# The first inner tile's weights loaded alone ahead of x's first tile, the second's behind it, and four idle products instead of five

## The chip, the core and the metric

The kernel runs on one core of one Trainium2 chip. The metric is the device time of one execution in microseconds (us). Five engines work side by side, each through its own fixed list of instructions and in that order: TensorE (PE; its weight loads are listed as PEld), VectorE (DVE), ScalarE (ACT), GpSimd (POOL) and SyncE (SP, which here only issues DMAs). They wait for each other with semaphores. TensorE's clock has two levels, 1.2 and 2.4 GHz.

## What is computed

One layer of a decoder over 1024 tokens of width 1024 in fp32. Only its beginning matters here:

```
h = _rmsnorm(r, attn_norm[i]).astype(dt)
z = h @ w_in[i]
aq, af, ai, ag, bq, bk, bv, cq, ck, cv, cg = jnp.split(z, SPLITS, axis=-1)
hd = lambda t: t.reshape(b, s, -1, HEAD_DIM)
ya = _hgrn2(hd(aq), hd(af), hd(ai), hd(ag), lb_all[i], hgrn_gnorm[i])
yb = _swa_sinks(hd(bq), hd(bk), hd(bv), attn_sinks[i], cos, sin)
yc = _retention(hd(cq), hd(ck), hd(cv), hd(cg), cos, sin)
...
r = r + mix @ w_out[i]
r = r + _conv_ffn(h2, w_gate[i], w_up[i], conv_w[i], conv_b[i], w_down[i])
```

`_hgrn2` is a gated linear recurrence over the tokens. Behind these come a gated per-layer embedding and a last norm.

## The kernel before

Every large fp32 product is made of three products of rounded halves (`mm3`, lines 113 to 117): weight high by x high (L115), weight high by x low (L116), weight low by x high (L117). A "high" half is a copy into the type fp32r, made by ACT; the "low" half is the difference, made by DVE. One product takes 128x128 weights against 512 tokens.

**The start.** The projection's columns are cut into 22 tiles (`FT`), of which the first three (af0, aq0, ai0) are computed while x arrives. x is transposed, eight inner tiles `x0` to `x7` of 128 x 1024, each loaded in two halves of 512 tokens (256 KB each) by SP. The weights of these three column tiles come in pairs of inner tiles (`w_first`, four DMAs of 384 KB, `wr_s0` to `wr_s6`), each ahead of its pair of x tiles on SP's queue. Of each x tile ACT makes `xh` (times the norm's gain, which lies in `small`, loaded on ACT's queue), DVE makes `xl`, ACT the squares for the norm, and TensorE then makes 18 products: 3 column tiles x 2 halves x 3. The order of the code within this loop is:

```
if k % 2 == 0:
    raw = ap.tile([P, 2, NS * P], F32, ...)
    nc.sync.dma_start(raw, a["w_first"][k // 2])
for h in range(2):
    nc.sync.dma_start(x[:, half(h)], a["xT"][k][:, half(h)])
if k % 2 == 0:
    wh, wl = split_w(raw, [P, 2, NS * P], f"s{k}")
for h in range(2):
    S.mul(hi[:, half(h)], x[:, half(h)], col(C_G1 + k))
```

Ahead of it TensorE multiplies a zeroed tile (`idle`, L209); one such fp32 product is two passes in the trace. A DMA takes one of eight semaphore lanes; an issuing engine waits until the lane's DMA before has landed.

**Behind it.** The sum of squares (`ss_x`) goes through a reciprocal root on DVE, is spread by TensorE (`rb_x`) and copied by ACT in two halves into `rs1` (L185). Then the other column tiles follow one by one (`project`, L254: load, `wh_` on ACT, `wl_` on DVE, 48 products), and between them the products of the recurrence (`hgrn`, from L437): seven levels n, each for two token halves h. A level's four products (`level`, L458, tiles `l{j}{n}{h}`, so `l011` is part 0, level 1, half 1) read `q` and `k`; then DVE selects the scores (L466), multiplies q (L482) and k (L483), and k so multiplied is what the next level of that half reads. The tables of the rotary embedding (`rope_tables`: L509 to L526, `ang`, `angn`, `sinT`, `cosT`) are laid between the levels. A product's result lies in one of three PSUM buffers (`pg`), which is free for the next column tile once DVE has read it.

The order on each engine comes from a scheduler with a model of its own that looks at the whole program; the code's order and priorities are its input.

Of the kernel before, what the change touches and what calls it, by code (L numbers as in the profile page):

```python
# [17 lines left out]
F32 = mybir.dt.float32  # L18
F32R = mybir.dt.float32r
# [3 lines left out]
ALU = mybir.AluOpType  # L23
# [3 lines left out]
P = 128  # L27
# [14 lines left out]
NS = 3  # L42
# [31 lines left out]
def trunk(ctx: ExitStack, tc: tile.TileContext, a, out, out_end, dbg):  # L74
    nc = tc.nc
    V, S, G, TE = nc.vector, nc.scalar, nc.gpsimd, nc.tensor
# [3 lines left out]
    wp = ctx.enter_context(tc.tile_pool(name="wp", bufs=2))  # L80
# [9 lines left out]
    def b1(name):  # L90
        return ps.tile([P, H2], F32, tag="b1", bufs=5, name=name)

    def half(h):
        return slice(h * H2, (h + 1) * H2)
# [5 lines left out]
    def split_w(raw, shape, name, e=V):  # L100
        hi = wp.tile(shape, F32R, tag="whi", bufs=2, name=f"wh_{name}")
        S.copy(hi, raw)
        lo = wp.tile(shape, F32R, tag="wlo", bufs=2, name=f"wl_{name}")
        e.tensor_tensor(out=lo, in0=raw, in1=hi.bitcast(F32), op=ALU.subtract)
        return hi, lo
# [7 lines left out]
    def mm3(o, wh, wl, xh, xl, first, last, on=False):  # L113

        TE.matmul(o, wh, xh, start=first, stop=False, skip_group_check=on)  # L115
        TE.matmul(o, wh, xl, start=False, stop=False, skip_group_check=on)  # L116
        TE.matmul(o, wl, xh, start=False, stop=last, skip_group_check=on)  # L117
# [8 lines left out]
    def col(i):  # L126
        return small[:, i:i + 1]
# [77 lines left out]
    idle = ap.tile([P, H2], F32, tag="st", bufs=2, name="idle")  # L205
    V.memset(idle, 0.0)
    pt = b1("idle")
    for _ in range(5):
        TE.matmul(pt[:, :256], idle[:, :P], idle[:, :256], start=True, stop=True)  # L209
    S.dma_start(small, a["small"])  # L210
    with tc.high_priority(offset=100000):
        xs = [ap.tile([P, T], F32, tag="zg", bufs=4, name=f"x{k}") for k in range(4)]
        xs += [ap.tile([P, T], F32, tag=t, bufs=1, name=f"x{4 + k}") for k, t in enumerate(("ob", "zo"))]
        both = ap.tile([P, 2, T], F32, tag="ob2", bufs=1, name="x67")
        xs += [both[:, k, :] for k in range(2)]
        for k in range(KD):
            x = xs[k]
            hi = big.tile([P, T], F32R, tag="big", name=f"xh{k}")
            lo = big.tile([P, T], F32R, tag="big", name=f"xl{k}")
            if k % 2 == 0:  # L220
                raw = ap.tile([P, 2, NS * P], F32, tag=("s0", "s1", "kt", "zt")[k // 2], bufs=1, name=f"wr_s{k}")
                nc.sync.dma_start(raw, a["w_first"][k // 2])
            for h in range(2):
                nc.sync.dma_start(x[:, half(h)], a["xT"][k][:, half(h)])
            if k % 2 == 0:
                wh, wl = split_w(raw, [P, 2, NS * P], f"s{k}")
            for h in range(2):
                S.mul(hi[:, half(h)], x[:, half(h)], col(C_G1 + k))
                V.scalar_tensor_tensor(out=lo[:, half(h)], in0=x[:, half(h)], scalar=col(C_G1 + k),
                                       in1=hi[:, half(h)].bitcast(F32), op0=ALU.mult, op1=ALU.subtract)  # L230
            if k == 0:
                S.square(acc, x)
            else:
                sq = ap.tile([P, T], F32, tag="zv", bufs=2, name=f"sq{k}")
                S.square(sq, x)
                V.tensor_tensor(out=acc, in0=acc, in1=sq, op=ALU.add)
            xh.append(hi)
            xl.append(lo)
            for n in range(NS):
                for h in range(2):  # L240
                    w = slice(n * P, n * P + P)
                    mm3(first[n][h], wh[:, k % 2, w], wl[:, k % 2, w], hi[:, half(h)], lo[:, half(h)],
                        k == 0, k == KD - 1)
# [166 lines left out]
    def hgrn_f(j, of):  # L410
        f = zt(f"f{j}", "zf", 1)
        k = zt(f"k{j}", "zk", 2)
        scaled(f, of)
        S.activation(k, f, AF.Sigmoid, scale=-1.0)
        S.activation(f, f, AF.Sigmoid)
        V.tensor_scalar(out=k, in0=k, scalar1=oml[:, j:j + 1], scalar2=None, op0=ALU.mult)
        V.tensor_scalar(out=f, in0=f, scalar1=oml[:, j:j + 1], scalar2=lbt[:, j:j + 1], op0=ALU.mult, op1=ALU.add)
        return f, k
# [293 lines left out]
    f, k = hgrn_f(0, first[0])  # L712
# [5 lines left out]
    f, k = got["af1"]  # L718
# [49 lines left out]
    def f4(tag, name, shape=(P, T), dt=F32):  # L768
        if tag == "big":
            return big.tile(list(shape), dt, tag="big", name=name)  # L770
        if tag in ("wraw", "whi", "wlo"):
            return wp.tile(list(shape), dt, tag=tag, bufs=1 if tag == "wraw" else 2, name=name)
        return fp.tile(list(shape), dt, tag=tag, bufs=BUFS[tag], name=name)
# [125 lines left out]
    def weights_up_1(f):  # L899

        if f == 1:
            g = cp.tile([P, T], F32, tag="rs", bufs=1, name="wg1")
        else:
            g = f4("ws" if f == 2 else "w5" if f > 2 and f % 2 else "wraw", f"wg{f}")
        nc.sync.dma_start(g.rearrange("p (k c) -> p k c", k=KD), a["w_gu"][f, 0])
        hi, lo = [f4(t, f"{t}g{f}", dt=F32R) for t in ("whi", "wlo")]
        hl(hi, lo, g)
        return g, {n + 1: (hi[:, half(n)], lo[:, half(n)]) for n in range(2)}
# [138 lines left out]
    with tc.high_priority(offset=3000):  # L1047
        raw, A0 = weights_up_1(0)
# [5 lines left out]
    with tc.high_priority(offset=3000):  # L1054
        raw, A1 = weights_up_1(1)
# [23 lines left out]
    for f in range(3, NF):  # L1079
        with tc.high_priority(offset=3000):  # L1080
            raw, A = weights_up_1(f)
# [190 lines left out]
    for n in range(NC // 2):  # L1272
# [7 lines left out]
        for i, (d0, d1) in enumerate(groups):  # L1280
# [8 lines left out]
            t = f4("big", f"et{n}{i}")[:, :d1 - d0]  # L1289
# [138 lines left out]
```

## Time and profile before

| | |
|---|---|
| median of 3 runs | 1246.35 us (1245.96 to 1246.54) |
| the profiled execution | 1246.38 us |
| its span, first to last instruction | 1244.6 us |
| TensorE busy | 1225.4 us, 98% of the span |
| VectorE busy | 892.2 us, 72% |
| ScalarE busy | 543.8 us, 44% |
| mean granted clock of TensorE | 0.998 of full speed |

Times in the trace count from the first instruction. "Idle before" an instruction and what ended it stand in brackets. In a row with xN, N instructions were merged, the duration runs from the first's start to the last's end, and the name loses its numbers (`z_af` is any half of af0 or af1).

### The profile page before, as it was taken

To read this page: it belongs to the slowest core of one execution; us is meant where nothing else is said; L and a number is where in the kernel's file an instruction comes from. 1 tells how busy PE (TensorE), PEld (TensorE's weight loads), DVE (VectorE), ACT (ScalarE), POOL (GpSimd) and SP (SyncE) were. 2 spreads that over 40 slices of the span, in tenths; PEclk is the share of its full clock that TensorE was granted. 3 is DMA by queue.
4 is the path that set the end of the run, shared out by engine and by line. 5 is a ranking of instruction groups with operands and counts; after the bars stand their busy time and mean duration, and the time that the engine had idled before them with its cause. 6 is when DMAs were issued, how large, how long until landed. Compare 5 with 4: busy or idle time off the path is not lost.

```text
span 1244.6 us, 15889 instructions
## 1 busy us (share of the span) xinstructions
PE 1225.4 (98%) x6030; PEld 1023.5 (82%) x6030; DVE 892.2 (72%) x1510; ACT 543.8 (44%) x838; POOL 126.7 (10%) x158
## 2 busy tenths in 40 slices
PE   9999999999999999999999999999999999999997
PEld 7888888887888888887788888888888888888886
DVE  7996967557777476987878887787667675566374
ACT  7324233247766344754343334433335353444332
POOL 2000000011210313100111111111101000000000
PEclk9999999999999999999999999999999999999999
DMA  7100110110001944333554544544579786443131
GB/s 258 51 23 29 35 34 18 34 34 34 24 29 46 353 127 166 121 94 127 177 177 152 179 130 154 182 160 154 191 265 339 272 290 207 144 152 119 34 135 68
DMA packets 59964, 165.53 MB, mean 133 GB/s; under 512 B 6320, under 2 KB 6832, under 8 KB 59888
## 3 DMA queue, kind: packets, MB, share of 16 engines
q1 hardware_dynamic: 42608, 106.71, 25.6%
q0 software_dynamic: 15552, 55.84, 13.2%
q10 hardware_dynamic: 1728, 1.97, 0.5%
q8 instruction: 47, 0.77, 0.3%
q14 instruction: 29, 0.24, 0.1%
HBM read 120.20 MB, written 44.30 MB: 132 GB/s over the span
## 4 chain that ended last, share of the span: by engine, by line
PE 51%; DVE 1%; DMA 0%; issue 0%; ACT 0%; DVEq 0%
PE d L116 6%; PE d L115 6%; PE d L117 6%; PE gb L116 5%; PE gb L117 5%; PE gb L115 5%; PE gd L117 3%; PE gd L115 3%; PE gd L116 3%; PE ga L116 1%; PE ga L117 1%; PE ga L115 1%; PE pe L117 1%; PE pg L115 1%; PE pe L115 1%; PE pe L116 1%
## 5 line engine op out<-in xcount | busy, mean ns | idle before, releaser
L115 PE MATMUL d<-hhd,hwd 128*128 128x512 f32 x308 | 119.8, 389 | 0.0
L116 PE MATMUL d<-lhd,hwd 128*128 128x512 f32 x308 | 119.8, 389 | 0.0
L117 PE MATMUL d<-hhd,lwd 128*128 128x512 f32 x308 | 119.8, 389 | 0.0
L781 DVE TENSOR_TENSOR lwd<-wdr,hwd 128x1024 fp32r<-128x1024 f32 (+1 forms) x39 | 47.0, 1209 | 36.9 <-ACT hwd L780 36.8
L780 ACT CAST hwd<-wdr 128x1024 fp32r<-128x1024 f32 (+1 forms) x39 | 40.5, 1039 | 72.8 <-PE d L116 59.0
L115 PE MATMUL gd<-b,f 128*128 128x512 f32 x176 | 68.8, 391 | 1.4 <-ACT us L964 1.4
L115 PE MATMUL gb<-b,hf 128*128 128x512 f32 x176 | 68.7, 390 | 0.1
L116 PE MATMUL gd<-b,f 128*128 128x512 f32 x176 | 68.5, 389 | 0.0
L117 PE MATMUL gd<-b,f 128*128 128x512 f32 x176 | 68.5, 389 | 0.0
L116 PE MATMUL gb<-b,hf 128*128 128x512 f32 x176 | 68.5, 389 | 0.0
L117 PE MATMUL gb<-b,lf 128*128 128x512 f32 x176 | 68.3, 389 | 0.0
L115 PEld LDWEIGHTS d<-hhd,hwd 128*128 128x128 f32 x308 | 57.8, 188 | 12.1
L117 PEld LDWEIGHTS d<-hhd,lwd 128*128 128x128 f32 x308 | 57.8, 188 | 12.1
L116 PEld LDWEIGHTS d<-lhd,hwd 128*128 128x128 f32 x308 | 57.8, 188 | 11.8
L781 DVE TENSOR_TENSOR lhd<-hr,hhd 128x1024 fp32r<-128x1024 f32 (+1 forms) x39 | 46.7, 1207 | 6.7 <-ACT hhd L780 6.5
L780 ACT CAST hhd<-hr 128x1024 fp32r<-128x1024 f32 (+1 forms) x39 | 39.8, 1034 | 20.1 <-DMA hr<-tad 11.0
L780 ACT CAST f<-wg 128x512 fp32r<-128x512 f32 x22 | 13.7, 624 | 77.7 <-PE gd L117 77.7
L781 DVE TENSOR_TENSOR f<-s,f 128x1024 fp32r<-128x1024 f32 x22 | 26.9, 1224 | 28.3 <-ACT f L780 28.3
L780 ACT CAST f<-s 128x1024 fp32r<-128x1024 f32 x22 | 23.1, 1050 | 50.3 <-PE gb L117 46.5
L115 PEld LDWEIGHTS gd<-b,f 128*128 128x128 f32 x176 | 33.0, 188 | 9.3 <-ACT us L964 2.5
L115 PEld LDWEIGHTS gb<-b,hf 128*128 128x128 f32 x176 | 33.0, 188 | 7.7 <-ACT gs L964 0.5
L971 DVE SCALAR_TENSOR_TENSOR cv<-gs,small,cv 128x1023 f32<-128x1023 f32 x22 | 28.2, 1284 | 15.1 <-ACT cv L970 15.1
(491 smaller groups left out, 3506.1 us busy)
## 6 DMA issues: line engine op xcount, KB each, us to landing
wg<-w_gu SPq DMA_DIRECT2D x22, 512.0 KB, 4.4
wu<-w_gu SPq DMA_DIRECT2D x22, 512.0 KB, 3.5
sd<-w_dn POOLq DMA_DIRECT2D x22, 512.0 KB, 5.2
sd<-sd POOLq DMA_DIRECT2D x22, 512.0 KB, 3.9
wdr<-sd SPq DMA_DIRECT2D x44, 256.0 KB, 3.7
wr_wo<-w_out SPq DMA_DIRECT2D x16, 512.0 KB, 3.7
wdr<-w_dn SPq DMA_DIRECT2D x15, 512.0 KB, 4.8
hod<-us POOLq DMA_DIRECT2D x11, 512.0 KB, 2.9
```

Of the source, the lines that this page charges most:

```text
L115: TE.matmul(o, wh, xh, start=first, stop=False, skip_group_check=on)
L116: TE.matmul(o, wh, xl, start=False, stop=False, skip_group_check=on)
L117: TE.matmul(o, wl, xh, start=False, stop=last, skip_group_check=on)
L780: S.copy(hi, src)
L781: return e.tensor_tensor(out=lo, in0=src, in1=hi.bitcast(F32), op=ALU.subtract)
L971: V.scalar_tensor_tensor(out=cv[:, 1:], in0=gs[:, :T - 1], scalar=w(1), in1=cv[:, 1:], op0=ALU.mult, op1=ALU.add)
```

## The change

Of the first pair of weights only tile 0's part (192 KB) is loaded ahead of `x0`, and tile 1's part ahead of `x1`; the high and low halves of these two parts are made apart, each at its own tile's turn. The other three pairs stay as they are. TensorE makes four idle products instead of five. From here on a line has a number that is nine higher.

```
-    for _ in range(5):
+    for _ in range(4):
         TE.matmul(pt[:, :256], idle[:, :P], idle[:, :256], start=True, stop=True)
...
+            if k < 2:
+                nc.sync.dma_start(raw[:, k, :], a["w_first"][0][:, k, :])
+            elif k % 2 == 0:
                 nc.sync.dma_start(raw, a["w_first"][k // 2])
             for h in range(2):
                 nc.sync.dma_start(x[:, half(h)], a["xT"][k][:, half(h)])
-            if k % 2 == 0:
+            if k == 0:
+                wh, wl = [wp.tile([P, 2, NS * P], F32R, tag=t, bufs=2, name=f"{t}_s0") for t in ("whi", "wlo")]
+            if k < 2:
+                S.copy(wh[:, k, :], raw[:, k, :])
+                V.tensor_tensor(out=wl[:, k, :], in0=raw[:, k, :], in1=wh[:, k, :].bitcast(F32), op=ALU.subtract)
+            elif k % 2 == 0:
                 wh, wl = split_w(raw, [P, 2, NS * P], f"s{k}")
```

The scheduler answers with other orders in a few places. At the start SP's list was (in brackets the lanes it waits for; `DMAHW0` is the lane of `small`, `DMAHW1` that of `wr_s0`):

```order
L222 DMA wr_s0_110<-w_first 128x768
L224 DMA x0_101<-xT 128x512 x2
L224 DMA x1_102<-xT 128x512 x2
L222 DMA wr_s2_172<-w_first 128x768 [waits DMAHW1_49]
L224 DMA x2_103<-xT 128x512 [waits DMAHW2_49]
```

and is now:

```order
L224 DMA wr_s0_109<-w_first 128x384
L228 DMA x0_100<-xT 128x512 x2
L224 DMA wr_s0_109<-w_first 128x384
L228 DMA x1_101<-xT 128x512
L228 DMA x1_101<-xT 128x512 [waits DMAHW0_49]
L226 DMA wr_s2_174<-w_first 128x768 [waits DMAHW1_49]
L228 DMA x2_102<-xT 128x512 [waits DMAHW2_49]
```

So x1's second half stands behind a wait for `small`. On TensorE the first products were:

```order
L209 MATMUL idle_94<-idle_92 128x256 x5
L115 MATMUL z_af00_85<-xh0_108,wh_s0_114 128x512
L116 MATMUL z_af00_85<-xl0_109,wh_s0_114 128x512
L117 MATMUL z_af00_85<-xh0_108,wl_s0_116 128x512
L115 MATMUL z_af01_86<-xh0_108,wh_s0_114 128x512
L115 MATMUL z_aq00_87<-xh0_108,wh_s0_114 128x512
L116 MATMUL z_aq00_87<-xl0_109,wh_s0_114 128x512
L117 MATMUL z_aq00_87<-xh0_108,wl_s0_116 128x512
L116 MATMUL z_af01_86<-xl0_109,wh_s0_114 128x512
```

and are now (`z_af00` is the first token half of af0, `z_af01` the second):

```order
L209 MATMUL idle_94<-idle_92 128x256 x4
L115 MATMUL z_af00_85<-xh0_107,whi_s0_113 128x512
L115 MATMUL z_af01_86<-xh0_107,whi_s0_113 128x512
L116 MATMUL z_af00_85<-xl0_108,whi_s0_113 128x512
L117 MATMUL z_af00_85<-xh0_107,wlo_s0_114 128x512
L115 MATMUL z_aq00_87<-xh0_107,whi_s0_113 128x512
L116 MATMUL z_af01_86<-xl0_108,whi_s0_113 128x512
```

The second product is now the one that needs the second half of `xh0`, ahead of the one that needs `xl0`. On ACT the mask `rmask` is issued some 20 rows later than before, and in the place behind the norm's sum the high half of af1's weights, which stood ahead of both copies into `rs1`, stands between them:

```order
L517 DMA posi_721<-pos 128x1024
L185 COPY rs1_70<-rb_x_410 128x512
L102 CAST wh_af1_443<-wr_af1_441 128x1024
L185 COPY rs1_70<-rb_x_416 128x512
L423 ACT_TABLE_LOAD
```

The third place is among the first levels of the recurrence. TensorE's list there was:

```order
L458 MATMUL l001_574<-q0_431,k0_424 128x128 x4
L458 MATMUL l010_596<-q0_431,k0_424 128x128 x3
L115 MATMUL z_aq11_539<-xh0_108,wh_aq1_534 128x512
...
L117 MATMUL z_aq11_539<-xh7_333,wl_aq1_536 128x512
L458 MATMUL l011_625<-q0_431,k0_424 128x128 x4
L458 MATMUL l020_635<-q0_431,k0_424 128x128 x4
L115 MATMUL z_ai10_651<-xh0_108,wh_ai1_647 128x512
```

and is now:

```order
L467 MATMUL l001_576<-q0_433,k0_426 128x128 x4
L467 MATMUL l010_598<-q0_433,k0_426 128x128 x4
L467 MATMUL l011_627<-q0_433,k0_426 128x128 x4
L115 MATMUL z_aq11_541<-xh0_107,wh_aq1_536 128x512
...
L117 MATMUL z_aq11_541<-xh7_335,wl_aq1_538 128x512
L467 MATMUL l020_637<-q0_433,k0_426 128x128 x4
L115 MATMUL z_ai10_653<-xh0_107,wh_ai1_649 128x512
```

`l011` has moved from behind the 24 products of `z_aq11` to ahead of them. DVE's list in that place is now (`k0` behind `l001` is what `l011` reads; the buffer that `z_aq11` takes is the one that the first `f1` row frees, where before it was the one that two `q1` rows ahead of `l001`'s selection freed):

```order
L475 COPY_PREDICATED sa01_507<-lmask_75,l000_554 128x256
L491 TENSOR_TENSOR q0_433<-q0_433,f0_425 128x512
L492 TENSOR_TENSOR k0_426<-k0_426,f0_425 128x256
L535 TENSOR_TENSOR sinT_385<-sinT_385,rs1_70 128x1024
L438 TENSOR_TENSOR q1_620<-z_aq10_540,rs1_70 64x512
L475 COPY_PREDICATED sa00_506<-lmask_75,l001_576 128x256
L475 COPY_PREDICATED sa01_507<-lmask_75,l001_576 128x256
L491 TENSOR_TENSOR q0_433<-q0_433,f0_425 128x512
L492 TENSOR_TENSOR k0_426<-k0_426,f0_425 128x256
L475 COPY_PREDICATED sa00_506<-lmask_75,l010_598 128x128x2
L299 TENSOR_TENSOR f1_497<-z_af10_447,rs1_70 128x512
```

Before, two `q1` rows stood in place of `sinT` and one `q1`, and `sinT` had come earlier. Two more moves on DVE lie ahead of this: of the four rows L516 (`ang`) two stood ahead of `f0` and two behind it, and now it is one and three; and `angn` (L522) stands ahead of `l000`'s selection now, not behind `l001`'s. Behind it, the rows `wl_ag0`, `cosT` and the two `q1` of `z_aq11` stood ahead of `l011`'s multiplication of `k0` and stand behind it now. From some 30 rows further on the engines' lists are the same.

## Rows read from the trace of the kernel before

**Rows 1.** The page's part 1: busy time, share of the span and number of instructions of each engine.

```profile
PE 1225.4 (98%) x6030; PEld 1023.5 (82%) x6030; DVE 892.2 (72%) x1510; ACT 543.8 (44%) x838; POOL 126.7 (10%) x158
```

**Rows 2.** The view of waits for TensorE over the whole span, one of its longest: who waited for whom, us in total, times, longest.

```profile
PE l L458 <- DVE k L483: 1.4, 2, 0.8
```

**Rows 3.** The timeline of the first 10 us: start, duration, engine (SPq and ACTq are the issue of DMAs), line, operation, out<-in. The first x row is x0's first half; the pair at 1.67 begins with x0's second half, the pair at 2.13 is x1's.

```profile
0.74 0.41 ACTq L210 DMA_DIRECT2D small<-small  x1
1.20 0.42 SPq L224 DMA_DIRECT2D x<-xT  x1
1.67 0.90 SPq L224 DMA_DIRECT2D x<-xT  x2
2.13 0.91 SPq L224 DMA_DIRECT2D x<-xT  x2
...
4.14 0.83 ACT L102 CAST wh_s<-wr_s 128x768 fp32r<-128x768 f32 x1 [1.46 <-DMA wr_s<-w_first]
5.14 0.72 ACT L228 ACTIVATE xh<-x,small 128x512 fp32r<-128x512 f32 x1 [0.17 <-DMA x<-xT]
5.91 0.50 PE L115 MATMUL z_af<-xh,wh_s 128*128 128x512 f32 x1 [0.46 <-ACT xh L228]
6.33 0.72 ACT L228 ACTIVATE xh<-x,small 128x512 fp32r<-128x512 f32 x1 [0.46 <-DMA x<-xT]
6.70 0.49 PE L116 MATMUL z_af<-xl,wh_s 128*128 128x512 f32 x1 [0.29 <-DVE xl L229]
7.04 0.40 PE L117 MATMUL z_af<-xh,wl_s 128*128 128x512 f32 x1
7.08 0.75 DVE L229 SCALAR_TENSOR_TENSOR xl<-x,small,xh 128x512 fp32r<-128x512 f32 x1 [0.43 <-ACT xh L228]
7.27 0.40 PE L115 MATMUL z_af<-xh,wh_s 128*128 128x512 f32 x1
```

**Rows 4.** From issue to landing, us: the DMAs issued around 0.7 to 1.25 us (KB each, last column), then x0's second half alone, then all of x's up to 20 us.

```profile
wr_s<-w_first SPq DMA_DIRECT2D x1, 384.0 KB, 3.4
x<-xT SPq DMA_DIRECT2D x1, 256.0 KB, 3.9
...
small<-small ACTq DMA_DIRECT2D x1, 62.0 KB, 3.6
...
DMA to landing us min/median/max: 4.6/4.6/4.6
...
DMA to landing us min/median/max: 3.9/5.5/6.1
```

**Rows 5.** A stretch of the start: from:to us, length, busy us of the engines, granted clock, DMA share, GB/s.

```profile
8.00:9.00 1.00, 1.00 (x6) 0.84 (x5) 0.35 (x1) 1.00 (x2) 0.00 (x0) 1.00 1.04 374
```

**Rows 6.** The passes of the idle products in narrow windows of the timeline; each row begins with the start of the first pass that runs in its window.

```profile
4.18 0.84 PE L209 MATMUL idle<-idle 128*128 128x256 f32 x2
4.61 0.84 PE L209 MATMUL idle<-idle 128*128 128x256 f32 x3
4.86 0.59 PE L209 MATMUL idle<-idle 128*128 128x256 f32 x2
```

**Rows 7.** The timeline of ACT and DVE behind the norm's sum.

```profile
32.85 1.04 ACT L102 CAST wh_af<-wr_af 128x1024 fp32r<-128x1024 f32 x1 [6.84 <-PE z_ai L116]
33.93 1.23 DVE L104 TENSOR_TENSOR wl_af<-wr_af,wh_af 128x1024 fp32r<-128x1024 f32 x1 [0.93 <-ACT wh_af L102]
34.18 0.59 ACT L185 COPY rs<-rb_x 128x512 f32<-128x512 f32 x1 [0.28 <-PE rb_x L173]
38.04 2.49 DVE L516 SCALAR_TENSOR_TENSOR ang<-angn,ang 128x1024 f32<-128x1024 f32 x2
42.59 1.37 DVE L290 TENSOR_TENSOR ai<-z_ai,rs 128x512 f32<-128x512 f32 x2 [0.27 <-PE z_ai L117]
```

**Rows 8.** The timeline of DVE at the first levels.

```profile
55.23 0.69 DVE L447 TENSOR_TENSOR sa<-l0d,ident 128x512 f32<-128x512 f32 x1 [1.41 <-PE l0d L446]
55.84 1.22 DVE L526 TENSOR_TENSOR sinT<-sinT,rs 128x1024 f32<-128x1024 f32 x1
63.91 0.41 DVE L483 TENSOR_TENSOR k<-k,f 128x256 f32<-128x256 f32 x1
64.24 1.38 DVE L429 TENSOR_TENSOR q<-z_aq,rs 64x512 f32<-64x512 f32 x2
67.41 0.41 DVE L483 TENSOR_TENSOR k<-k,f 128x256 f32<-128x256 f32 x1
```

**Rows 9.** The timeline of TensorE in the same stretch (the number behind the x counts passes: an fp32 product has two; a product's start to the next one's is its pace).

```profile
60.07 1.15 PE L458 MATMUL l<-q,k 128*128 128x128 f32 x8 [0.23 <-DVE q L472]
63.80 1.75 PE L458 MATMUL l<-q,k 128*128 128x128 f32 x14
65.77 0.47 PE L115 MATMUL z_aq<-xh,wh_aq 128*128 128x512 f32 x1 [0.22 <-DVE q L429]
73.31 0.48 PE L115 MATMUL z_ai<-xh,wh_ai 128*128 128x512 f32 x1
78.90 1.16 PE L458 MATMUL l<-q,k 128*128 128x128 f32 x8 [0.79 <-DVE k L483]
81.64 0.47 PE L115 MATMUL z_ai<-xh,wh_ai 128*128 128x512 f32 x1
```

**Rows 10.** The view of waits for DVE from 380 to 604 us, its longest row.

```profile
DVE r L827 <- PE o L117: 29.6, 10, 3.4
```

## The prediction

> **What bounds the kernel now.** I read the page's busy shares first, then TensorE's waits, then the timelines at the places where the order of instructions differs. TensorE is busy for 1225.4 of 1244.6 us [rows 1], so the time is that of its list plus its waits: about 19 us, of which some 6 lie ahead of the first product that counts. The longest later one is short: 1.4 us in two waits for DVE's multiplication of k [rows 2]. What moves TensorE's stream therefore moves the end, unless a later wait shrinks or grows with it. In the start the reader is to see three steps: the weights land and are cast at 4.14, x0's first half lets `xh` start at 5.14 and the first product at 5.91, x0's second half lets `xh` start only at 6.33 [rows 3]. From the third product at 7.04 on the stream runs without a gap, one product in 0.23 us (7.04 to 7.27). The tiles behind are no limit: 18 products take 18 x 0.227 = 4.1 us, a tile of x and its weights (704 KB) at the 374 GB/s of [rows 5] 1.9 us.
>
> **The start, part by part.** (1) *192 KB less ahead of x0.* x0's second half was issued at 1.67 and landed 4.6 later, at 6.27 [rows 3, 4]. How much earlier it lands no row shows. Upper bound: the first half landed at 5.1 (issued at 1.20, plus 3.9), 0.95 behind the weights' 4.14; at that pace 192 KB are worth 0.71 us. Lower bound: nothing, if the 4.6 us are a latency of issue. By the rate of 374 GB/s they are 196.6 / 374 = 0.53. I take 0.55, since the rate is that of a busy queue and this queue is busy: 5.72. From `xh`'s start to its product took 0.77 (5.14 to 5.91), and 0.06 lay between landing and start (6.27 to 6.33), so the product that needs the second half of `xh0` can run at 5.72 + 0.06 + 0.77 = 6.55. It now stands second on TensorE, so the third comes 0.34 later (6.70 to 7.04 in rows 3) at 6.89, against 7.04. **Gain 0.15.** `xl0` of the first half is ready before that: `xh` moves from 5.14 to about 4.6, product and `xl` with it, since the smaller cast (384 columns for 768, half of 0.83 us) ends at about 4.1; `small` lands at 0.74 + 3.6 = 4.34 [rows 3, 4] and is no later. The sixth product needs `xl0` of the second half: `xh` ends at 6.50, `xl` takes 0.75, 7.28; TensorE comes there at 6.89 + 3 x 0.23 = 7.58. The bounds give the third product at 6.73 (gain 0.31) and at 7.44 (loss 0.40). A loss is possible since before only the fourth product needed that half, and three ran ahead of it.
>
> The Trainium skill's page "DMA: Bandwidth & Descriptors", section "Anatomy of one DMA — SWDGE (gpsimd) path", puts a DMA at a fixed part of about 2 us plus its bytes at 436 GB/s, with the fixed part mostly the wait for the last write's receipt. By it 196.6 KB less are worth 0.45 us and the gain of the start would be 0.05; my 0.55 goes by this case's rows.
>
> (2) *The second part of the weights ahead of x1, and x1's second half behind a wait.* SP issued all of x1 by 2.13 + 0.91 = 3.04 [rows 3]; now the second half waits for `small`, 4.34. With the 3.9 to 6.1 us of [rows 4] it lands at 8.3 to 10.4. Its `xh` is wanted by the fourth product of the next tile, 6.89 + 15 x 0.227 + 0.23 + 3 x 0.23 = 11.2, its `xl` at 11.5: landing by about 9.9 hides it. Cost 0, at most 0.5. What SP issues behind it waits for lanes that free earlier than before (weights, x0), and `rmask`'s 256 KB leave this stretch.
>
> (3) *Four idle products.* Their passes start 0.43 apart to 4.61, then 0.25 [rows 6]: the step from 1.2 to 2.4 GHz falls between, while the eighth pass (the fourth product's last) runs. Four products reach to about 5.0, so the step still falls into them; 0.
>
> **Behind the norm's sum.** Now `rs1`'s first copy, 34.18 to about 34.7, precedes the cast of `wh_af1`, which stood at 32.85. So `wl_af1` moves from 33.93 to 34.7 + 1.04 + 0.04 = 35.8, DVE is 1.85 late [rows 7]. One L516 less ahead of `f0` gives back 1.2, the 0.27 us wait ahead of `ai` the most of a third: 0.3 late. TensorE wants `wh_af1` only after 36 products from 34.8 on, at 43: hidden, with 6 us to spare. The third L516 behind `f0` adds 1.14.
>
> **The levels.** DVE finished the preparations at 53.8 (55.23 less the wait of 1.41) and will do so at 53.8 + 0.3 + 1.14 = 55.25. There it no longer waits for TensorE, and neither the first `sa` nor `sinT` (1.13) stand ahead of `wl_ai`: `wl_ai` 1.14, two `sa` 1.2, q 1.13, two `sa` 1.2, q 1.13, `angn` 0.6, selection 1.09 and q 0.65 bring it to `k0` of `l000` at 63.4 (63.91 before). Then `sinT` 1.13 and one `q1` 0.61 stand where two `q1` took 1.42, so `k0` behind `l001`, which started at 67.41 and took 0.41, starts at about 67.2 and ends at 67.6 [rows 8]. **Unchanged, but wanted earlier**: `l011` reads it, and stands now right behind `l010`. TensorE comes there early: `l000` no longer waits (60.07 becomes 59.7), 12 products from 60.6 end at 63.4, `l001` and `l010` at 0.215 a product end at 65.15. **`l011` waits 2.45 us**, to 67.6, and ends at 68.5; `z_aq11` waits further until the first `f1` has freed its buffer (67.55, selection 0.55, `f1` 0.69): 68.8 for 65.77 [rows 9].
>
> What comes back: 24 products without the odd `l010` take 5.6 us, to 74.4, then 4 products of `l020` (0.86) instead of 8 bring `z_ai10` to 75.3, for 73.31: 2.0 late. At 78.90 TensorE waited 0.79 us for `k0` of `l011`, behind a DVE that had `cosT`, `wl_ag0` and two `q1` ahead of it; these stand behind it now, it ends at about 75.0, and `l021` starts at 75.3 + 2.8 = 78.1 with no wait. `l021` 0.87, 12 products 2.83, `l030` 0.85: `z_ai11` at 82.65, for 81.64. **Loss 1.0.** Both chains hang on TensorE's start alike, so the 0.15 stays a term of its own. Behind 90 us the lists are the same, and DVE waits for TensorE again and again (ten times for `o` alone, 29.6 us [rows 10]), so a shift of TensorE shifts its partners; later waits give nothing back.
>
> **Sum.** Against the profiled execution's own 1246.38 us (span 1244.6, 1.78 around it; median of the runs 1246.35): 1246.38 - 0.15 + 1.0 = 1247.2 us.
>
> **Rivals.** (A) *The forecast*, 55%. (B) *x0's second half lands no earlier*, the 4.6 us being latency: loss 0.4 in the start, 1247.8. For it: it landed 1.17 behind the first half, while the weights were 0.95 ahead of that. Against: the queue is full. 14%. (C) *DVE is ahead at the levels*: were it over 2.5 us earlier, `l011` would not wait, `z_aq11`'s wait would go too, and the 0.23, 0.22 and 0.79 us of waits in [rows 9] would be partly gone: some 0.7 less than before, and with the 0.15 of the start 1245.5. Against: DVE has 1.41 us of waiting to give in that stretch and 1.14 of new work ahead of it. 16%. (D) *DVE is a microsecond later* (the cast of `wh_ai1`, or `sinT` waiting for ACT): it comes in full, 1248.2. 9%. (E) *The clock falls back*: with one idle product less TensorE does one product between 5.0 and 6.55, and if that cost it the upper level, products take twice 0.227 us; from about seven such products on (7 x 0.23 = 1.6 us on top of the forecast) the kernel is slower by over 0.2%. With eight: 1247.2 + 1.8 = 1249.0. Against: before it stood 0.46 and 0.29 us without a loss of pace. 6%. The page "TensorE: Matmul & The Clock Gate", section "What's actually happening" in the Trainium skill, says the clock is held down by default and released by activity; by it (E) is possible, and the pace of [rows 6] agrees that activity released it here.
>
> **Numbers.** Runs of one kernel spread here by 0.6 us; 0.2% is 2.5 us, which is what a measurement can tell from no change. Predicted: 1247.2 (A). The range from 1245.4 to 1248.5 takes in A to D with their bounds and leaves out E and the ends. Faster by over 0.2% (under 1243.9): 2%, what C with both upper bounds would still miss. Slower (over 1248.9): 7%, E and the end of D. Within 0.2%: 91%.
>
> **What would show it.** Right: the third product at about 6.9; the cast of the first weights near 3.6; a wait of about 2.4 us of `l011` for DVE's k near 65 and a short one of `z_aq11` for `f1`; no wait at `l021`; `z_ai11` about 0.85 later than 81.64; the same waits as before behind 90 us. Wrong: a third product behind 7.04 (B), a pace over 0.23 there (E), no wait at `l011` (C), or later waits that shrink by what was lost.

## The result, and the profile after

| | before | after |
|---|---|---|
| median of 20 runs each | 1246.53 us (1245.61 to 1249.91) | 1248.12 us (1246.52 to 1252.08) |
| span of the profiled execution | 1244.6 us | 1246.2 us |
| ratio after to before | | 1.0015, 95% interval 1.0009 to 1.0021 |

The changed kernel is 1.6 us slower, within 0.2%. The forecast was 1247.2 us, so 0.8 us of loss was seen ahead and 0.8 was not. TensorE has as much work as before [rows 1]: two passes fewer, and 1.4 us more that a slower pace at the start makes. The new wait is the one that was forecast: 2.3 us in place of the longer of the two waits that make up the 1.4 us of [rows 2]; the other, 0.65 at 140 us, is still there. The page's part 1 and the view of TensorE's waits (us in total, times, longest):

```profile
PE 1226.8 (98%) x6028; PEld 1024.8 (82%) x6028; DVE 892.4 (72%) x1511; ACT 543.7 (44%) x839; POOL 126.7 (10%) x158
```

```profile
PE l L467 <- DVE k L492: 3.0, 2, 2.3
```

The start in the timeline (start, duration, engine, line, operation, out<-in; in brackets the idle time ahead and what ended it), the counterpart of [rows 3]:

```profile
3.46 0.51 ACT L232 CAST whi_s<-wr_s 128x384 fp32r<-128x384 f32 x1 [0.78 <-DMA wr_s<-w_first]
4.47 0.72 ACT L237 ACTIVATE xh<-x,small 128x512 fp32r<-128x512 f32 x1 [0.50 <-DMA x<-xT]
5.24 0.80 PE L115 MATMUL z_af<-xh,whi_s 128*128 128x512 f32 x1
5.54 0.72 ACT L237 ACTIVATE xh<-x,small 128x512 fp32r<-128x512 f32 x1 [0.35 <-DMA x<-xT]
6.32 0.79 PE L115 MATMUL z_af<-xh,whi_s 128*128 128x512 f32 x1 [0.28 <-ACT xh L237]
6.91 0.63 PE L116 MATMUL z_af<-xl,whi_s 128*128 128x512 f32 x1
7.34 0.63 PE L117 MATMUL z_af<-xh,wlo_s 128*128 128x512 f32 x1
...
9.47 0.63 PE L117 MATMUL z_aq<-xh,wlo_s 128*128 128x512 f32 x1
9.90 0.47 PE L115 MATMUL z_aq<-xh,whi_s 128*128 128x512 f32 x1
10.20 0.40 PE L116 MATMUL z_aq<-xl,whi_s 128*128 128x512 f32 x1
10.44 0.39 PE L117 MATMUL z_aq<-xh,wlo_s 128*128 128x512 f32 x1
```

Loads and casts are earlier, as meant: the second half's `xh` starts at 5.54 for 6.33. But from 6.91 to 9.90 the seven products stand 0.43 us apart, where before they stood 0.23 apart from 7.04 on [rows 3]. Products stand as far apart where the clock column reads 0.50 (69.68 to 70.11 in the second run with five idle products, below), so this is the pace of the lower of the two clock levels, and 7 x 0.2 = 1.4 us of loss. The third product at 6.91 looks like the forecast's 6.89, but by the pace of [rows 3] (0.34 behind the second) it would have been 6.66. The view by stretches does not show the lower level here: its clock column (the 1.00 ahead of the DMA share) is as high as in [rows 5], yet x3 stands where x6 stood:

```profile
8.00:9.00 1.00, 1.00 (x3) 0.76 (x3) 0.93 (x3) 1.00 (x3) 0.00 (x0) 1.00 0.98 363
```

The levels on TensorE, against [rows 9], with the very last product:

```profile
61.03 1.07 PE L467 MATMUL l<-q,k 128*128 128x128 f32 x8
64.68 1.98 PE L467 MATMUL l<-q,k 128*128 128x128 f32 x16
68.96 1.15 PE L467 MATMUL l<-q,k 128*128 128x128 f32 x8 [2.31 <-DVE k L492]
70.02 0.50 PE L115 MATMUL z_aq<-xh,wh_aq 128*128 128x512 f32 x1
76.41 0.48 PE L115 MATMUL z_ai<-xh,wh_ai 128*128 128x512 f32 x1
79.25 1.05 PE L467 MATMUL l<-q,k 128*128 128x128 f32 x8
83.70 0.48 PE L115 MATMUL z_ai<-xh,wh_ai 128*128 128x512 f32 x1
...
1237.14 0.28 PE L117 MATMUL pe<-hpg,lp 128*128 128x256 f32 x1
```

And DVE, against [rows 7, 8]:

```profile
37.09 1.23 DVE L104 TENSOR_TENSOR wl_af<-wr_af,wh_af 128x1024 fp32r<-128x1024 f32 x1 [2.29 <-ACT wh_af L102]
...
68.41 0.40 DVE L492 TENSOR_TENSOR k<-k,f 128x256 f32<-128x256 f32 x1
69.25 1.31 DVE L299 TENSOR_TENSOR f<-z_af,rs 128x512 f32<-128x512 f32 x2
```

This splits the profiled difference. Ahead of the levels TensorE is 1.19 us late (61.03 against 60.07 less its wait of 0.23). Behind them `z_ai11` is 2.06 late (83.70 against 81.64), so **the levels cost 0.87**. The last product (1235.13 before) is 2.01 late: nothing is given back in between. The tail behind it, on other engines, was 0.4 shorter in this execution, which leaves the 1.6 of the spans. So 1.2 us are the start's, where the forecast had a gain of 0.15. The rows of the kernel before for the norm's sum and for the last product are:

```profile
29.05 1.84 PE L159 MATMUL ss_x<-ones,acc 128*128 128x1 f32 x16
...
1235.13 0.28 PE L117 MATMUL pe<-hpg,lp 128*128 128x256 f32 x1
```

### The profile page after: what moved, and what is told of

Read it like the earlier page. It is cut to its first block, busy times and chain, and to the rows that moved or that the text cites. A ratio compares the mean times of both kernels' runs of the same rounds, so it can differ in the third digit from the quotient of the medians.

```text
span 1246.2 us, 15891 instructions
## 1 busy us (share of the span) xinstructions
PE 1226.8 (98%) x6028; PEld 1024.8 (82%) x6028; DVE 892.4 (72%) x1511; ACT 543.7 (44%) x839; POOL 126.7 (10%) x158
## 4 chain that ended last, share of the span: by engine, by line
PE 51%; DVE 1%; DMA 0%; issue 0%; ACT 0%; DVEq 0%
PE d L117 6%; PE d L116 6%; PE d L115 6%; PE gb L115 5%; PE gb L117 5%; PE gb L116 5%; PE gd L115 3%; PE gd L117 3%; PE gd L116 3%; PE ga L115 1%; PE ga L117 1%; PE ga L116 1%; PE pe L117 1%; PE pg L115 1%; PE pe L115 1%; PE pe L116 1%
```

## The experiments

Three theories stood open. *Clock*: with the fifth idle product gone, TensorE reaches its upper level later. *Order*: the loss is that of `l011` ahead of `z_aq11`. *Clock at the wait*, which came up with the first profiles: behind `l011`'s wait the clock falls in some executions, and the wait costs more than its length. Each ratio below is to runs of the kernel before on the same chip.

**One idle product less, alone, and one more.** The first edit is the change's own with nothing else moved; the second goes the other way.

```
-    for _ in range(5):
+    for _ in range(4):
```

> The kernel before with four idle products instead of five, and nothing else; every engine's list stays as it was. Clock theory (with one idle product less TensorE's upper level comes later, as the pace of 0.43 us a product from 6.9 to 9.9 us in the changed kernel's trace suggests): the first products behind 5.9 us run at 0.43 us each until about 10 us, some 7 of them by then instead of 14, so about 1.4 us slower than before, 1248.0. Order theory (all of the loss is the levels' order, the idle products cost nothing): within 0.3 us of before, 1246.5.

> The kernel before with six idle products; every other list as before. The sixth makes TensorE busy until about 5.9 us at the higher level, when the first product is ready anyway. Clock theory: with five the upper level came at 4.7 to 6.5 us in the executions profiled, so there is little left to gain: 0 to 0.3 us faster than before, 1246.2 to 1246.5. If each idle product were worth what the fifth was: 0.8 faster.

Measured: 1247.30 us with four, against 1246.45 (ratio 1.0006, 0.9997 to 1.0015); 1246.22 with six, against 1246.50 (1.0002, 0.9993 to 1.0011). By the times alone neither differs from five. The timeline of TensorE with four:

```profile
9.74 0.40 PE L117 MATMUL z_af<-xh,wl_s 128*128 128x512 f32 x1
9.98 0.39 PE L115 MATMUL z_aq<-xh,wh_s 128*128 128x512 f32 x1
...
30.39 1.84 PE L159 MATMUL ss_x<-ones,acc 128*128 128x1 f32 x16
```

Here too the pace reaches 0.23 (9.74 to 9.98) only near 10 us, and the norm's sum begins 1.34 late, at 30.39 as in the changed kernel. So the late rise and its price up to the sum are seen without the split loads. The price in the kernel's time, 0.85 by the medians and 0.59 by the means, is not settled by these runs.

The end of one profile can't settle it either. TensorE was still 1.33 us late in this execution at `z_ai11` (82.97 for 81.64), but only 0.48 at the last product, since a wait far behind the edits was missing. In the kernel before it is:

```profile
603.50 0.50 PE L115 MATMUL gd<-b,f 128*128 128x512 f32 x1 [0.94 <-ACT us L964]
```

The wait comes and goes between executions of one kernel: of the two profiles with five idle products below, the first lacks it and the second has it at 0.97, as the changed kernel's has. Seven of the fourteen profiles lack it or have 0.27 at most of it; in six of these, 0.72 to 0.85 us of what TensorE had lost by `z_ai11` is given back at the end (the seventh has another wait, of 1.40 near 590 us).

**The fifth idle product back in the changed kernel, twice.**

> The changed kernel with the fifth idle product put back; every list but for that product as in the changed kernel. Clock theory: the first products run at 0.23 us, the third product starts at 6.6 to 6.7 us (0.3 to 0.4 ahead of before, since x0's second half lands earlier), the wait of l011 stays and costs 0.6 to 0.9: 1246.5 - 0.35 + 0.75 = 1246.9, about 1.2 us faster than the changed kernel. Order theory: no faster than the changed kernel, 1248.1.

> The changed kernel with five idle products a second time, as the mate of the next two. Clock-at-the-wait theory (in some executions TensorE's clock falls behind the 2.3 us in which l011 waits, as it did in the profiled execution of the kernel before with l011 moved ahead, 3.4 us at 0.50 from 67.9 on): the times stand in two groups again, one near 1246.3 and one near 1248.3, median about 1248. Wait-only theory (the wait costs what the timeline shows and no more): one group.

Measured: 1248.08 us (1.0008, 0.9999 to 1.0017) and 1248.13 us (1.0012, 1.0004 to 1.0021): by the medians no faster than the changed kernel, against the clock theory's 1246.9. The two groups of times stand apart in the first run (four up to 1246.69, seven from 1247.97), and not clearly in the second. Yet the two profiled executions have the upper level by the third product. DVE and TensorE in the first of them:

```profile
9.47 0.75 DVE L238 SCALAR_TENSOR_TENSOR xl<-x,small,xh 128x512 fp32r<-128x512 f32 x1 [0.61 <-ACT xh L237]
```

```profile
6.48 0.39 PE L116 MATMUL z_af<-xl,whi_s 128*128 128x512 f32 x1
...
29.16 1.92 PE L159 MATMUL ss_x<-ones,acc 128*128 128x1 f32 x16 [0.51 <-DVE acc L245]
...
67.83 1.14 PE L467 MATMUL l<-q,k 128*128 128x128 f32 x8 [2.32 <-DVE k L492]
...
70.38 0.40 PE L115 MATMUL z_aq<-xh,wh_aq 128*128 128x512 f32 x1
```

The third product is 0.56 earlier than before, but `ss_x`, the norm's sum, now waits 0.51 us for DVE's additions into `acc` and starts no earlier than before (29.16; before, it began at 29.05 without a wait). In the second execution DVE met no pause at x1's second half, and TensorE none at the sum; there the clock fell behind `l011` instead. DVE, TensorE, and the view by stretches of TensorE (from:to, length, busy, then the granted clock):

```profile
8.05 1.41 DVE L238 SCALAR_TENSOR_TENSOR xl<-x,small,xh 128x512 fp32r<-128x512 f32 x2
```

```profile
28.45 1.84 PE L159 MATMUL ss_x<-ones,acc 128*128 128x1 f32 x16
...
67.02 1.58 PE L467 MATMUL l<-q,k 128*128 128x128 f32 x8 [2.30 <-DVE k L492]
...
69.68 0.63 PE L115 MATMUL z_aq<-xh,wh_aq 128*128 128x512 f32 x1
70.11 0.63 PE L116 MATMUL z_aq<-xl,wh_aq 128*128 128x512 f32 x1
...
70.96 0.41 PE L115 MATMUL z_aq<-xh,wh_aq 128*128 128x512 f32 x1
```

```profile
67.00:68.00 1.00, 0.98 (x7) 0.78 0.00 0
68.00:69.00 1.00, 1.00 (x5) 0.50 0.00 0
...
70.00:71.00 1.00, 1.00 (x4) 0.51 0.00 0
71.00:72.00 1.00, 1.00 (x6) 1.00 0.00 0
```

From `l011`'s start to the seventh product behind it, 2.55 us pass with the clock up (67.83 to 70.38) and 3.94 with it down (67.02 to 70.96): **a fall costs 1.4 us**, more than the 0.87 that the levels cost without it.

**The order at the levels alone, both ways.** DVE's two `q1` rows free the buffer of `z_aq11`; their priority decides which product the scheduler puts first. The first edit (with five idle products) brings the old order into the changed kernel, the second (offset -600) the new order into the kernel before.

```
-                V.tensor_tensor(out=q[r, h, hd, :], in0=o[h][r], in1=rs1[r, half(h)], op=ALU.mult)
+                with tc.high_priority(offset=100 if j == 1 else 0):
+                    V.tensor_tensor(out=q[r, h, hd, :], in0=o[h][r], in1=rs1[r, half(h)], op=ALU.mult)
```

> The changed kernel with five idle products, and the rows that make q1 out of z_aq1 on DVE 100 steps up in priority: both of the first half stand ahead of l001's selection again, and TensorE's list has l011 behind the 24 products of z_aq11 as before. If the order at the levels costs 0.6 to 0.9: that much faster than the changed kernel with five idle products, 1246.1 to 1246.2, and 0.3 to 0.4 faster than before. If the order costs nothing: as the changed kernel with five idle products.

> The kernel before with its start (weights of a pair together, five idle products) and the rows that make q1 600 steps down in priority: l011 then stands ahead of z_aq11 on TensorE, as in the changed kernel. If the order at the levels costs what the forecast says: a wait of l011 of 2 to 2.5 us, no wait at l021, and 0.6 to 1.0 us slower than before, 1247.1 to 1247.5. If all of the loss is the start's: 1246.5.

Measured: 1246.33 us with the old order in the changed kernel (0.9996, 0.9987 to 1.0005), 1.75 less than with the new one; 1247.81 us with the new order in the kernel before (1.0012, 1.0003 to 1.0021). So the order carries a loss by itself, by the medians (1.36 and 1.75) more than the forecast's 1.0, though the intervals reach below that. That order has a price in the first kernel too: in its profile `z_aq11` waits 0.97 us for its `q1` rows, and the levels cost 0.43 against the kernel before. In the second kernel's profile the clock fell once more:

```profile
67.59 1.77 PE L459 MATMUL l<-q,k 128*128 128x128 f32 x8 [1.93 <-DVE k L484]
```

```profile
68.00:69.00 1.00, 1.00 (x7) 0.50 0.00 0
```

**The wait filled.** Eight products nobody reads go ahead of `l011`, into its own buffer; nothing is left out of the computation.

```
+            if (j, n, h) == (0, 1, 1):
+                for _ in range(8):
+                    TE.matmul(pt, xh[0][:, :P], xh[0][:, half(0)], start=True, stop=True)
-            for c in range(4):
+            with tc.high_priority(offset=400 if (j, n, h) == (0, 1, 1) else 0):
+                for c in range(4):
```

> The changed kernel with five idle products, and eight products of xh0 with itself into l011's own buffer just ahead of l011's four, which overwrite them: 8 x 0.23 = 1.85 us of work for nothing inside the wait of 2.3 us; l011 starts when it did. Clock-at-the-wait theory: the group near 1248.3 goes, median 1246.5 to 1246.9, over 1 us less than without the eight. Wait-only theory: the same median as without them, 1248.0, or later by what they overrun.

> The kernel before with l011 moved ahead of z_aq11, a second time, as the mate of the next one. Clock-at-the-wait theory: 1247.5 to 1248 as the first time, with some times near 1246.3 and the most of them near 1248. Wait-only theory: the same median, since it makes no difference here.

> The same with the eight products of xh0 with itself ahead of l011's four. The wait's own price of 0.6 to 0.9 us stays, since l011 starts when it did. Clock-at-the-wait theory: no clock fall behind l011, and 0.5 to 1.5 us less than without the eight, 1246.5 to 1247.3. Wait-only theory: no less than without them, 1247.8.

> The changed kernel itself (four idle products) with the same eight products ahead of l011. It stands against the run with five idle products and the eight: if the missing idle product leaves TensorE at the lower level until about 10 us in most executions, 0.8 to 1.3 us slower than that run, about 1247.7; if the idle products cost nothing, the same.

Measured, without and with the eight on the same chip: 1248.13 and 1246.44 us in the changed kernel with five idle products (with them 1.0003, 0.9995 to 1.0012); 1248.24 (1.0014, 1.0006 to 1.0023) and 1247.15 (1.0008, 0.9999 to 1.0017) in the kernel before with the new order. Of all 44 times without the eight in these two kernels 26 are 1247.9 us or more, of the 22 with them four; the mean is 0.82 us less (95% interval 0.32 to 1.31, by drawing the times again). TensorE with them, in the changed kernel and then in the kernel before:

```profile
66.61 2.09 PE L467 MATMUL l<-xh 128*128 128x512 f32 x8
69.10 1.18 PE L471 MATMUL l<-q,k 128*128 128x128 f32 x8 [0.40 <-DVE k L496]
```

```profile
66.18 2.09 PE L459 MATMUL l<-xh 128*128 128x512 f32 x8
68.30 1.17 PE L463 MATMUL l<-q,k 128*128 128x128 f32 x8
```

`l011` still starts when DVE's k is there, and the kernel is faster for doing more work: the wait-only theory falls. No profile with the eight has a fall at this place (four profiles); of the five without them that have the wait, three do. Taken as in the changed kernel (`z_ai11` against what stood ahead of `l000`), the levels cost 0.83 to 0.94 us in the six of these profiles without a fall, filled or not, and 2.21 to 2.29 in the three with one. The mean granted clock, on record for 260 executions, agrees: it is 0.996 or less in 20 of the 64 whose kernel has the unfilled wait, and in 5 of the 196 others. What the filled kernel of the second pair still loses, 0.75 us of median, is of the size of the order's own 0.87.

The changed kernel itself with the eight (four idle products) took 1247.21 us (1.0004, 0.9995 to 1.0013), 0.77 more than with five by the medians, near what the clock theory expected. But the means are only 0.37 us apart (95% interval -0.36 to 1.10), so this does not show it, and in its profile the upper level was there by the third product although there were only four:

```profile
6.63 0.40 PE L116 MATMUL z_af<-xl,whi_s 128*128 128x512 f32 x1
6.87 0.40 PE L117 MATMUL z_af<-xh,wlo_s 128*128 128x512 f32 x1
```

**x1 whole.** One DMA for x1 takes one lane less, so that SP no longer waits for `small`.

```
+            if k == 1:
+                nc.sync.dma_start(x, a["xT"][k])
+            else:
-            for h in range(2):
-                nc.sync.dma_start(x[:, half(h)], a["xT"][k][:, half(h)])
+                for h in range(2):
+                    nc.sync.dma_start(x[:, half(h)], a["xT"][k][:, half(h)])
```

> The run with five idle products and q1 first, with x1 loaded by one DMA of 512 KB instead of two of 256 KB: SP then issues all of x1 without the wait for small. TensorE's list has four more products ahead of the norm's sum. DVE theory (VectorE works without a pause from x1 to the norm's sum, so the 0.4 to 0.7 us that it waits for x1's second half come out at the sum, and TensorE's earlier start is given back there): that wait of DVE goes, the last addition into acc ends 0.4 to 0.7 us earlier, TensorE does not wait at the norm's sum, and the kernel is about 0.5 us faster than with x1 in two parts, 1245.8, which would be 0.6 faster than before. Rival (the pause of DVE is slack): 1246.3 as without the edit.

> The run with five idle products and the eight products in l011's wait, with x1 loaded by one DMA. DVE theory: no wait of DVE for x1's second half, no wait of TensorE ahead of the norm's sum (0.64 us without the edit), and l011's k on DVE earlier by as much, since DVE's chain to the levels hangs on the sum: 0.4 to 0.6 us faster than without the edit, 1245.9. Rival (the pause is slack): 1246.4.

Measured: 1246.13 us (1.0, 0.9992 to 1.0009) and 1246.95 us (1.0008, 0.9999 to 1.0017), for 1246.33 and 1246.44 without the edit, on other chips (there 0.9996 and 1.0003). The 0.5 us do not show. Both profiles have TensorE's wait at the sum gone, and the second has DVE's pause gone:

```profile
8.40 1.42 DVE L241 SCALAR_TENSOR_TENSOR xl<-x,small,xh 128x512 fp32r<-128x512 f32 x2
```

```profile
29.68 1.84 PE L159 MATMUL ss_x<-ones,acc 128*128 128x1 f32 x16
```

But in the first a pause of 0.36 us is left, perhaps because x1's first half now comes only with the second; the sum has four more products ahead of it, and both profiles have a later wait of 1.3 us (`gb`, near 917 us) that no other profile has. Inconclusive. No version here is shown to beat the kernel before.

## Why the prediction was right, and where it was not

**The time lies in the range by the range's width, which is luck.** Of the 1.6 us of loss 0.8 were forecast, and the upper end of 1248.5 comes from rivals B and D, neither of which happened. The level term was sound, the start term had the wrong sign (1.2 us of loss in the profile for a gain of 0.15), and the extra price of a wait had no term at all.

**Levels: right.** `l011` waited 2.31 us (forecast 2.45), for DVE's k, which ended at 68.81, 1.2 behind the forecast's 67.6, by as much as TensorE came late from the start. `z_aq11` followed at once where a short wait for `f1` was expected. `l021` had no wait, and the stage cost 0.87 for 1.0. No later wait gave it back (2.06 to 2.01), but only because both profiled executions have the wait near 604 us: where it was missing or short, up to 0.85 came back.

**Behind the norm's sum: right.** `wl_af1` moved to 37.09, which is 35.8 and the start's delay, and TensorE had no wait for it.

**Four idle products at nothing: wrong.** The step argued that the clock rises while the eighth pass runs, so that four products contain it. That was read from one execution [rows 6]. In the changed kernel's trace the eighth pass starts at 4.61 as well, and the lower level's pace goes on behind it to 9.90:

```profile
4.61 0.64 PE L209 MATMUL idle<-idle 128*128 128x256 f32 x1
```

Over the profiles with five idle products the pace of 0.23 began between 4.86 and 7.45 us; with four it began at 6.63, 9.74 and 10.20. The moment differs between executions, and what the fifth product buys is a better chance, as far as three profiles with four can tell. This is the loss that rival E priced, at 6%, by another route: E had the clock fall back, and here it had not risen. It struck seven products, not eight. The Trainium skill's page "TensorE: Matmul & The Clock Gate", section "What's actually happening", says that the same kernel shows different numbers of slow products from run to run; the traces agree (with four idle products, seven slow ones behind the second in the changed kernel and none with the eight in the wait). The prediction cited that section and passed over this sentence.

**The landing: right, its worth: wrong.** The second half's `xh` started at 5.54, forecast 5.78, so rival B falls. It is 0.79 us earlier than before, more than the 0.55 of the sum and more than the 0.45 given beside it, which is for DMAs that GpSimd issues; these are SP's. But of the five profiled executions that have the split loads, x1 in two parts and the upper level by the third product, TensorE waited 0.27 to 0.64 us at the norm's sum in four. The step at fault is (2), which put x1's second half at no cost (0.5 at most) since TensorE wants its `xl` only at 11.5. DVE wants it at once: in the first execution with five idle products, after a last wait of 0.2 us at `acc`'s first addition, it works without a pause up to the sum, so its wait of 0.61 at 9.47 comes out at `ss_x`. The 0.15 was to be had only where DVE moved too: in the second execution, without that pause, DVE's last addition started 0.59 earlier than before (26.99 for 27.58) and the sum 0.60 (28.45 for 29.05). Removing the pause by an edit brought no timed gain, so this rests on the rows.

**What stays open.** How much of the time is the fifth idle product's. With the old order or with the wait filled it is worth 0.8 us of median (0.59 and 0.37 by the means); in the changed kernel as it stands nothing by the medians (1248.12 with four, 1248.08 and 1248.13 with five), but 0.65 by the means (95% interval -0.04 to 1.41). The intervals allow either. That executions which start late miss the fall behind `l011` more often, as the profiled one did, is not borne out: the mean clock is 0.996 or less in 9 of 20 with four idle products and in 6 of 22 with five.

## What to carry to other kernels

A stall of the busiest engine is not only as long as it looks: priced from one trace it was 0.87 us, in the runs of the order alone it was 1.4 and 1.8 us by the medians, and the rows show why: the clock fell behind it in some executions. Where an order can't be had that avoids the wait, products into a buffer that is overwritten anyway cover it: 0.82 us less by the mean here. A gain at the start is worth nothing if another engine works without a pause up to the next meeting point: look there first. Take a clock's step from several executions, never from one, and price an edit by the stage it touches: the end of one profile also holds waits that come and go.

## What the runs showed of the hardware that was not expected

- TensorE's clock fell to the lower level behind waits of 1.93 us (two executions) and 2.30 us (one; granted 0.50 in the rows above, 1.00 again in the stretch from 71 us), but not behind the 2.31 and 2.32 us of two other executions.
- It fell also near 32 us, behind the norm's sum, in two of the executions that waited there (0.29 and 0.64 us), and not in those with 0.27 and 0.51. The stretch in the changed kernel with five idle products and the eight:

```profile
32.00:33.00 1.00, 1.00 (x5) 0.61 0.00 0
...
34.00:35.00 1.00, 1.00 (x7) 0.50 0.00 0
```

- In the first 10 us the clock column reads 1.00 while the products run at the lower level's pace (0.43 us each); only the distance between starts tells.
